# Moving the rotary tables, the decays' sums and two gate columns in a hybrid decoder layer

## The chip, the cores and the metric

The kernel runs on one core of a Trainium2 chip. The metric is device time in microseconds (us) of one execution; lower is better. A core has five engines that work in parallel, each through a queue of its own in order: TensorE (PE: matmuls, with weight loads PEld), VectorE (DVE), ScalarE (ACT), GpSimd (POOL) and SyncE (SP), which here issues the DMA transfers. They wait for each other by semaphores. SBUF is the memory on the chip, PSUM the small memory into which TensorE writes, DRAM the large one outside.

## The reference

One layer on 1024 tokens of width 1024, in float32:

```
h = rms_norm(x, norm_w)
a_q, a_k, a_v, a_gate, b_q, b_k, b_v, b_gate, b_low, m_a, m_b = split(h @ w_in)
o_a = sliding_window_attention(rope(a_q), rope(a_k), a_v, sinks) * silu(a_gate)
y_a = o_a @ w_a_proj
log_a = log_sigmoid(b_low @ b_gate_up + b_gate_bias) / 16
o_b = gated_linear_attention(b_q, b_k, b_v, log_a)    # chunks of 64
y_b = (rms_norm(o_b, b_out_norm_w) * silu(b_gate)) @ w_b_proj
merged = sigmoid(m_a) * y_a + sigmoid(m_b) * y_b
out = rms_norm(x + merged @ w_out, final_norm_w)
```

In linear attention the queries are multiplied by exp of the running sum of log_a in a chunk, and the keys by exp of minus that sum.

## The kernel before

**Matmuls.** Every float32 operand is split into a high part (`fp32r`, a cast on ACT, L117) and a low part (a subtraction, L118, mostly on POOL), and a product is three matmuls per block of 128: high x high, high x low, low x high (`half_product`, L129). A *column* below is 128 columns of a weight. One column over all 1024 tokens is done either directly (`m_tiles`, L332: two halves of 512 tokens, 8 blocks, 3 matmuls: 48 matmuls of 128x512), or two columns together as a *pair* (`pair`, L598, and `seven_products`, L455), after Strassen and Winograd: seven products of 12 matmuls, 84, in place of 96. A pair adds and subtracts blocks of the raw weights on DVE first (the pre-adds, L467 to L470), then casts (ACT) and subtracts (POOL) each combination, while products 1, 2 and 6 use raw blocks. Products go to six PSUM banks `sj`; DVE and ACT add them up (c, u: L489, L506, L515, L531), and `emit` finishes a block. For the right-hand side, the pair needs four sums of blocks of the tokens' matrix, T1 to T4, split by `t_split` (L287).

**The order of the program.** A scheduler moves instructions within limits by its own model of time; `tc.issue_after(x)` forbids issuing before x, and `tc.high_priority` puts work ahead. By stages:

1. Token tiles (L210): norm, transposes, splits; beside them the first columns 0 to 2 of the merge gate A (`O_MA`). `rstd_of` (L144) makes 1/sqrt(ss/n + eps) with two POOL instructions: a scaling, and a power of -0.5.
2. T splits, the low-rank product `low` (L355), and column 3 of merge gate A directly (`m_tiles([3])`, L377).
3. Pairs (L640 to L653). First four of merge gate B (`O_MB`), each with the decay gates of a head (`log_gate`, L576: log-sigmoid on ACT, a scan on DVE, L590), whose running sums go to DRAM, `sp_cum` (L595). Behind the second pair's gates the rotary tables are traced (`rotary_tables`, L383): some 40 steps of 128x256 on DVE, two sines on ACT, twelve stores to `sp_rope`. Then the pairs of q and k of linear attention (each with a load of the sums, an exp on ACT, L630, into one of four buffers `gt`, and a multiplication on POOL, L631), of the gate and of the values.
4. Attention. Its outputs go to DRAM, `sp_oa`.
5. Linear attention by steps (`gla_step`, L881, one head and 128 tokens each): `gla(0)` for two heads, then `gla(2)`. Beside them stand *fillers*, independent matmuls for a waiting TensorE: columns 4 to 7 of merge gate A, of which two run at attention's end and two in `gla(0)`. The list `pace` ties each group of three filler matmuls to a step. In the same stretch attention's outputs are read back (`oraw`) and split.
6. Both projections. That of linear attention is four turns k of seven products; `merge` (L1084) makes the merged blocks c11 to c22 at their end, and these are split (`split_block`, L976) as right-hand sides `mt` of the last product, the first being mt[0] = c21.
7. The output projection, residual, and last norm (`finish`, L1107).

Of the kernel before, what the change touches and what calls it, by code (L numbers as in the profile page):

```python
# [69 lines left out]
def layer_kernel(ctx: ExitStack, tc: tile.TileContext, consts, x, positions, norm_w, w_in, a_sinks,  # L70
# [30 lines left out]
    sp_cum = spill.tile([BH * BK, T], F32, name="sp_cum")  # L101
# [42 lines left out]
    def rstd_of(pool, ss, n, width):  # L144
        r = pool.tile([P, width], F32, name="rstd")
        nc.gpsimd.tensor_scalar(r, ss, 1.0 / n, EPS, ALU.mult, ALU.add)  # L146
        nc.gpsimd.tensor_tensor(r, r, mhalf[:, :width], ALU.pow)
        return r
# [21 lines left out]
    mhalf = const.tile([P, 8], F32, name="mhalf")  # L170
# [115 lines left out]

    def t_split(i, tag):  # L287

        m = [tph.tile([P, 4, 512], F32R, name=f"t{i}h"), slot(tpl if tag else tph, tag or "tl")]
        r = tr[i - 1]  # L290
        for k in range(4):
            nc.scalar.copy(m[0][:, k, :], r[:, k, :])
            nc.vector.tensor_sub(m[1][:, k, :], r[:, k, :], f(m, 0, k))
        return m
# [46 lines left out]
    fillers = list(range(4, 8))  # L341
# [25 lines left out]
    caus = const.tile([P, P], I32, name="caus")  # L367
    nc.vector.tensor_copy(caus, le)
# [206 lines left out]
    decays = [mwork, sctx.enter_context(pool_of(name="ex", bufs=2))]  # L575
    def log_gate(hd, th):  # L576
# [5 lines left out]
        gx = up_.tile([P, 512], F32, name="u3")  # L582
# [12 lines left out]
        nc.sync.dma_start(sp_cum[hd * BK : hd * BK + BK, sl], gx)  # L595
        return scan.ins
# [19 lines left out]
    def keep(sp, row, mode=None):  # L616
        def emit(c, a, th, b):
# [7 lines left out]
            elif mode in ("up", "down"):  # L625
                decays.reverse()
                t = decays[0].tile([P, 512], F32, name="gt")
                r = row + a * P
                nc.sync.dma_start(t, sp_cum[r : r + P, th * 512 : th * 512 + 512])
                nc.scalar.activation(t, t, AF.Exp, scale=1.0 / 16.0 if mode == "up" else -1.0 / 16.0)  # L630
# [305 lines left out]
    pace += [steps[min(15, 2 + i // 2)] for i in range(16 * len(fillers))]  # L936
# [39 lines left out]
    def split_block(m, k, r):  # L976
        nc.scalar.copy(m[0][:, k, :], r)
        nc.vector.tensor_sub(m[1][:, k, :], r, f(m, 0, k))  # L978
# [72 lines left out]
    def sums(i):  # L1051
# [11 lines left out]
        if i == 6:  # L1063
            split_block(mt[0], 3, c21[3])
            sum_row(3)
            split_block(mt[5], 3, t1s[3])
        if i == 7:
# [110 lines left out]
```

## Time and profile before

| | us |
|---|---|
| runs of the kernel | 1079.79, 1079.21, 1076.34; median 1079.21 |
| profiled execution | 1076.43 |
| its span in the trace | 1074.6 |
| TensorE busy | 1027.0 (96%) |
| VectorE busy | 756.3 (70%) |
| ScalarE busy | 540.8 (50%) |
| GpSimd busy | 507.3 (47%) |

The time of an execution is the span of the trace and a little around it. Busy time counts an engine's instructions; a TensorE that is busy need not be at its peak, since its clock can be granted at half rate, which the rows by stretch show as "PEclk" (1.00 is full). In a row of waits, "A <- B" means that A's engine was idle before A until B was done.

### The profile page before, as it was taken

The numbers are of one execution on the slowest core, as the hardware profiler recorded it, in microseconds if no ns is written. First come the engines' busy times: TensorE is split into PE (matmuls) and PEld (weight loads), VectorE is DVE, ScalarE is ACT, GpSimd is POOL, SyncE is SP. The second block draws the span as 40 slices with busy tenths as digits, with TensorE's granted clock in tenths as the row PEclk, the third lists the DMA queues.
The fourth block names the chain that finished last, engine by engine and source line by source line (L and its number), as shares of the span: only waits on it lengthen the run. The fifth ranks groups of instructions, "written<-read, shape, count | busy, mean of one in ns | idle before, by whom it ended". The sixth has DMA issues, their size and how long they took to land.

```text
span 1074.6 us, 16232 instructions
## 1 busy us (share of the span) xinstructions
PE 1027.0 (96%) x5572; PEld 872.0 (81%) x5572; DVE 756.3 (70%) x1315; ACT 540.8 (50%) x1321; POOL 507.3 (47%) x438
## 2 busy tenths in 40 slices
PE   7999998989999999999999999989989999997996
PEld 5788866867889998888888888878778887786996
DVE  6984797444665332379988787878856388899786
ACT  6535576333343223466766667647655244244445
POOL 3034444778897444766678676747843100000002
PEclk9999999989999999999999999999999999999999
DMA  8413343444333317222222222429764388442415
GB/s 275 113 59 108 128 137 123 153 141 136 101 109 108 118 40 216 59 59 59 71 59 59 78 71 76 140 84 303 244 222 158 115 268 256 136 140 97 167 52 194
DMA packets 126260, 140.54 MB, mean 131 GB/s; under 512 B 10337, under 2 KB 87009, under 8 KB 126178
## 3 DMA queue, kind: packets, MB, share of 16 engines
q1 hardware_dynamic: 126178, 139.51, 41.1%
q8 instruction: 44, 0.72, 0.3%
q14 instruction: 38, 0.31, 0.1%
HBM read 94.52 MB, written 40.24 MB: 125 GB/s over the span
## 4 chain that ended last, share of the span: by engine, by line
PE 61%; DVE 9%; POOL 2%; ACT 2%; issue 2%; DMA 2%; SPq 0%; POOLq 0%; DVEq 0%; ACTq 0%
PE pj L134 25%; PE sj L134 13%; PE sj L452 13%; PE sc L765 2%; PE av L805 2%; PE av L849 2%; PE pt L789 1%; DVE b L978 1%; PE sc L849 1%; PE av L889 1%; DMA oraw<-sp_oa 1%; PE av L890 1%; PE pt L922 1%; DVE wl L118 1%; DVE sm L788 1%
## 5 line engine op out<-in xcount | busy, mean ns | idle before, releaser
L134 PE MATMUL pj<-o,wh 128*128 128x512 f32 x1072 | 348.2, 399 | 2.2 <-DVE o L228 1.6
L134 PEld LDWEIGHTS pj<-o,wh 128*128 128x128 f32 x1072 | 198.7, 190 | 42.9 <-DVE o L228 2.0
L134 PE MATMUL pj<-o,wl 128*128 128x512 f32 x536 | 213.2, 398 | 0.0
L118 POOL TENSOR_TENSOR wl<-sraw,wh 128x512 fp32r<-128x512 f32 (+1 forms) x98 | 155.5, 1604 | 111.8 <-ACT wh L117 105.1
L134 PEld LDWEIGHTS pj<-o,wl 128*128 128x128 f32 x536 | 101.1, 189 | 21.0
L134 PE MATMUL sj<-o,wh 128*128 128x512 f32 x352 | 111.2, 395 | 1.6 <-DVE o L489 0.8
L117 ACT CAST wh<-wr 128x1024 fp32r<-128x1024 f32 (+1 forms) x76 | 66.4, 890 | 78.4 <-PE sj L452 22.4
L117 ACT CAST wh<-sraw 128x512 fp32r<-128x512 f32 (+1 forms) x98 | 63.4, 678 | 83.7 <-PE sj L134 22.4
L146 POOL TENSOR_SCALAR rstd<-zs 128x1 f32<-128x1 f32 x8 | 2.7, 334 | 210.1 <-DVE zs L1110 209.7
L118 POOL TENSOR_TENSOR wl<-wr,wh 128x1024 fp32r<-128x1024 f32 x26 | 64.1, 2467 | 66.4 <-ACT wh L117 66.4
L506 DVE TENSOR_TENSOR u<-u,sj 128x512 f32<-128x512 f32 x48 | 32.9, 685 | 68.8 <-PE sj L134 35.6
L134 PEld LDWEIGHTS sj<-o,wh 128*128 128x128 f32 x352 | 65.7, 187 | 18.2 <-ACT u L515 1.3
L134 PE MATMUL sj<-o,wl 128*128 128x512 f32 x176 | 69.4, 394 | 0.0
L452 PE MATMUL sj<-wh,b 128*128 128x256 f32 x320 | 60.8, 291 | 6.0 <-DVE b L978 4.2
L134 PE MATMUL sj<-t,wh 128*128 128x512 f32 x144 | 57.6, 400 | 0.0
L489 DVE TENSOR_TENSOR c<-u,sj 128x512 f32<-128x512 f32 x48 | 32.7, 682 | 34.9 <-PE sj L134 10.5
L452 PEld LDWEIGHTS sj<-wh,b 128*128 128x128 f32 x320 | 51.8, 199 | 6.7 <-DVE b L978 4.4
L452 PE MATMUL sj<-wh,o 128*128 128x256 f32 x320 | 55.9, 278 | 1.3 <-DVE o L569 1.3
L780 ACT ACTIVATE sm<-sc,nm 128x129 f32<-128x129 f32 x128 | 45.8, 369 | 22.5 <-DVE nm L776 22.1
L797 POOL TENSOR_TENSOR ch<-ph,cst 128x512 fp32r<-128x512 f32 x32 | 37.1, 1158 | 40.4 <-ACT ph L796 32.9
L118 DVE TENSOR_TENSOR wl<-wr,wh 128x512 fp32r<-128x512 f32 (+1 forms) x50 | 45.4, 924 | 14.3 <-ACT wh L117 14.2
L452 PEld LDWEIGHTS sj<-wh,o 128*128 128x128 f32 x320 | 48.8, 188 | 1.6 <-DVE o L569 1.5
(316 smaller groups left out, 2707.0 us busy)
## 6 DMA issues: line engine op xcount, KB each, us to landing
sraw<-in_w_in_dram SPq DMA_DIRECT2D x32, 512.0 KB, 3.9
wr<-in_w_in_dram SPq DMA_DIRECT2D x26, 512.0 KB, 3.9
r<-sp_ob SPq DMA_DIRECT2D x28, 256.0 KB, 4.3
qs<-q SPq DMA_DIRECT2D x72, 64.0 KB, 2.0
xt<-in_x_dram SPq DMA_DIRECT2D x8, 512.0 KB, 8.1
sp_ma<-gt SPq DMA_DIRECT2D x16, 256.0 KB, 2.4
sp_mb<-c SPq DMA_DIRECT2D x16, 256.0 KB, 2.0
gt<-sp_cum SPq DMA_DIRECT2D x16, 256.0 KB, 3.4
```

Of the source, the lines that this page charges most:

```text
L117: nc.scalar.copy(h, raw)
L118: rest[0].tensor_sub(l, raw, h.bitcast(F32))
L134: nc.tensor.matmul(p, a[:, k, :], b[:, k, :], start=start and k == 0 and y == 0, skip_group_check=True, stop=stop and k == 3 and y == 2)
L452: nc.tensor.matmul(p, m[i][:, k, t * P : t * P + P], w[j][:, k, :], start=start and k == 0 and y == 0, skip_group_check=True, stop=stop an ...
L489: nc.vector.tensor_add(o, like(u[i][b], o), like(x[j][b], o))
L506: nc.vector.tensor_add(o[b], u[i][b], x[j][b])
L765: nc.tensor.matmul(s[:, h * 256 : h * 256 + 256], lq, kk[kv][x][:, k0 : k0 + 2, :].rearrange("p n t -> p (n t)"), start=x == 0, stop=x == 1)
L780: nc.scalar.activation(sm[:, j, :], sel[j // 2][:, j % 2, :], AF.Exp, bias=nm[:, j : j + 1], accum_out=den[:, j : j + 1])
L788: nc.vector.tensor_scalar_mul(sm[:, j, :P], sm[:, j, :P], den[:, j : j + 1])
L797: nc.gpsimd.tensor_mul(ch, ph.bitcast(F32), leb)
L805: nc.tensor.matmul(av[:, b * 256 : b * 256 + 256], val[:, blk, kv, :], part[:, 2 * b : 2 * b + 2, :], start=y == 0, stop=y == len(terms) - 1)
L849: nc.tensor.matmul(p, a[i], b[j], start=start and y == 0, stop=stop and y == 2)
```

## The change

- **Rotary tables.** They are issued after the last of the T splits, so in DVE's queue they stand at the first pair; their pool is freed there.
- **Decays' sums.** They stay in SBUF (`cum0` to `cum3`). Eight stores and sixteen loads go, and so does the second pool of `gt` buffers: two are left of four.
- **Merge gate A.** `m_tiles([3])` goes; the fillers are columns 3, 4 and 5 (two at attention's end, one in `gla(0)`), and columns 6 and 7 are a pair between the pairs of merge gate B and those of q and k. Direct matmuls ahead of attention: 48 fewer; a pair's: 84 more; fillers: 192 to 144. `low` is traced ahead of three half columns. `pace` advances by 3/4 of a step for each filler group rather than 1/2.
- **rstd.** The scaling is folded into the square's scale and an extra column that holds eps, for the token tiles and for the last norm; linear attention keeps it.
- **The mask.** `caus` is the bits of `le` in place of a cast.
- **End of the b projection (k = 3).** The merge of c21 and the split of mt[0] get high priority; the merge of c22 and the splits of mt[6] are issued after that split.

```
@@
-    def rstd_of(pool, ss, n, width):
-        r = pool.tile([P, width], F32, name="rstd")
-        nc.gpsimd.tensor_scalar(r, ss, 1.0 / n, EPS, ALU.mult, ALU.add)
-        nc.gpsimd.tensor_tensor(r, r, mhalf[:, :width], ALU.pow)
+    def power(pool, ss):
+        r = pool.tile([P, 1], F32, name="rstd")
+        nc.gpsimd.tensor_tensor(r, ss, mhalf, ALU.pow)
         return r
@@
+        for xt in xts:
+            nc.gpsimd.memset(xt[:, D:], (EPS * D) ** 0.5)
@@
-            nc.scalar.activation(junk, xt, AF.Square, accum_out=ss)
-            r = rstd_of(xp, ss, D, 1)
+            nc.scalar.activation(junk, xt, AF.Square, scale=D**-0.5, accum_out=ss)
+            r = power(xp, ss)
@@
-            nc.vector.tensor_sub(m[1][:, k, :], r[:, k, :], f(m, 0, k))
+            last_split.append(nc.vector.tensor_sub(m[1][:, k, :], r[:, k, :], f(m, 0, k)).ins)
@@
-    fillers = list(range(4, 8))
+    fillers = [3, 4, 5]
@@
-    caus = const.tile([P, P], I32, name="caus")
-    nc.vector.tensor_copy(caus, le)
+    caus = le.bitcast(I32)
@@
-    m_tiles([3])
@@
+    with tc.issue_after(last_split[-1]):
+        rotary_tables()
@@
-    decays = [mwork, sctx.enter_context(pool_of(name="ex", bufs=2))]
+    cums = gctx.enter_context(pool_of(name="cum", bufs=1, side="right"))
+    cum = [cums.tile([P, T], F32, name=f"cum{i}") for i in range(BH)]
@@
-        gx = up_.tile([P, 512], F32, name="u3")
+        gx = cum[hd][:, sl]
@@
-        nc.sync.dma_start(sp_cum[hd * BK : hd * BK + BK, sl], gx)
@@
-                decays.reverse()
-                t = decays[0].tile([P, 512], F32, name="gt")
-                r = row + a * P
-                nc.sync.dma_start(t, sp_cum[r : r + P, th * 512 : th * 512 + 512])
-                nc.scalar.activation(t, t, AF.Exp, scale=1.0 / 16.0 if mode == "up" else -1.0 / 16.0)
+                t = mwork.tile([P, 512], F32, name="gt")
+                nc.scalar.activation(t, cum[row // P + a][:, th * 512 : th * 512 + 512], AF.Exp, scale=1.0 / 16.0 if mode == "up" else -1.0 / 16.0)
                 nc.gpsimd.tensor_mul(c, c, t)
@@
-        if c == 2:
-            with tc.issue_after(scan):
-                rotary_tables()
+    pair(O_MA + 6 * P, P, keep(sp_ma, 6 * P, "tanh"))
@@
-    pace += [steps[min(15, 2 + i // 2)] for i in range(16 * len(fillers))]
+    pace += [steps[min(15, 2 + i * 3 // 4)] for i in range(16 * len(fillers))]
@@
-            split_block(mt[0], 3, c21[3])
+            with tc.high_priority(offset=400):
+                first.append(split_block(mt[0], 3, c21[3]))
+            with tc.issue_after(first[0]):
+                late.pop()()
@@
-            for k in range(4):
-                split_block(mt[6], k, c12[k])
+            with tc.issue_after(first[0]):
+                for k in range(4):
+                    split_block(mt[6], k, c12[k])
@@
         def merge(o, a, th, b):
+            if (k, a, th) == (3, 1, 1):
+                late.append(lambda: merge_block(o, a, th))
+                return
+            with tc.high_priority(offset=400) if (k, a, th) == (3, 1, 0) else nullcontext():
+                merge_block(o, a, th)
+
+        def merge_block(o, a, th):
@@
-    ssq = zw.tile([P, NT, 4], F32, name="ssq", bufs=1)
+    ssq = zw.tile([P, NT, 5], F32, name="ssq", bufs=1)
+    nc.gpsimd.memset(ssq[:, :, 4], EPS)
```

How the queue of VectorE reads in the third pair before (pre-adds of the weights `sraw`, sums c and u of the pair, and steps of the tables between them):

```order
L467 TENSOR_TENSOR sraw<-sraw 128x4x128
L531 TENSOR_TENSOR c<-u_1248,u_1283 128x512
L398 TENSOR_SCALAR rnd<-turns 128x256
L468 TENSOR_TENSOR sraw<-sraw 128x4x128
L506 TENSOR_TENSOR u_1214<-u_1214,sj 128x512
L489 TENSOR_TENSOR c<-u_1283,sj 128x512
L399 TENSOR_SCALAR rnd<-rnd 128x256
L469 TENSOR_TENSOR sraw<-sraw 128x4x128
L400 TENSOR_TENSOR turns<-turns,rnd 128x256
```

In that place only pre-adds, sums and gates are left. VectorE's queue now, at the start of the first pair, right behind the splits (the last step of `low`, then the pair's pre-adds, and the tables' `ang`, `dig` and `turns`):

```order
L382 CAST ang<-pos 128x256
L365 TENSOR_TENSOR low<-av,low 32x512
L470 TENSOR_TENSOR sraw<-sraw 128x4x128
L383 TENSOR_SCALAR ang<-ang,cst 128x256
L471 TENSOR_TENSOR sraw<-sraw 128x4x128
L387 TENSOR_SCALAR dig_709<-ang 128x256
L472 TENSOR_TENSOR sraw<-sraw 128x4x128
L388 TENSOR_SCALAR dig_709<-dig_709 128x256
L473 TENSOR_TENSOR sraw<-sraw 128x4x128
L389 SCALAR_TENSOR_TENSOR ang<-dig_709,ang 128x256
```

The tables' first steps moved between the first pair's pre-adds, and most of the others stand ahead of the pair's first c.

VectorE's queue before at the end of the b projection, where the last blocks are merged (`o_9490` is c12, `o_9492` c22, `o_9491` c21, `o_9489` c11) and split:

```order
L1091 TENSOR_TENSOR o_9492<-o_9492,yt 128x512
L978 TENSOR_TENSOR b_10153<-o_9492,b_10152 128x512
L1091 TENSOR_TENSOR o_9491<-o_9491,yt 128x512
L489 TENSOR_TENSOR o_9490<-u_10091,sj 128x512
L118 TENSOR_TENSOR wl<-wr,wh 128x1024
L978 TENSOR_TENSOR o_10216<-o_9490,o_10215 128x512 x3
L978 TENSOR_TENSOR b_10181<-o_9489,b_10180 128x512
L1090 SCALAR_TENSOR_TENSOR o_9490<-ym,o_9490 128x512
L978 TENSOR_TENSOR b_10038<-o_9491,b_10037 128x512
```

The last of these rows is the split of mt[0]. The same place now, with other numbers of the tiles (`o_9480` is c12, `o_9482` c22, `o_9481` c21, `o_9479` c11; the split of mt[0] is `b_10028`):

```order
L1103 TENSOR_TENSOR o_9481<-o_9481,yt 128x512
L977 TENSOR_TENSOR b_10137<-o_9482,b_10136 128x512
L492 TENSOR_TENSOR o_9480<-u_10081,sj 128x512
L117 TENSOR_TENSOR wl<-wr,wh 128x1024
L977 TENSOR_TENSOR b_10165<-o_9479,b_10164 128x512
L1102 SCALAR_TENSOR_TENSOR o_9480<-ym,o_9480 128x512
L977 TENSOR_TENSOR b_10028<-o_9481,b_10027 128x512
L1102 SCALAR_TENSOR_TENSOR o_9482<-ym,o_9482 128x512
L977 TENSOR_TENSOR o_10206<-o_9480,o_10205 128x512 x3
L470 TENSOR_TENSOR wr<-wr 128x1024
```

The three splits of `o_10206` (mt[6]) and the two merge steps of `o_9482` moved from ahead of mt[0]'s split to behind it.

More of the change, by code (lines that the diff above doesn't have):

```diff
@@ L98, in layer_kernel @@
     psum["pj"] = pj
-    sp_cum = spill.tile([BH * BK, T], F32, name="sp_cum")
     sp_oa = spill.tile([D, T], F32, name="sp_oa")
@@ L169, in layer_kernel @@
     le = cst[:, C_LE : C_LE + P]
-    mhalf = const.tile([P, 8], F32, name="mhalf")
+    mhalf = const.tile([P, 1], F32, name="mhalf")
     nc.gpsimd.memset(mhalf, -0.5)
@@ L191, in layer_kernel @@
         nc.vector.memset(ones[:, :1], 1.0)
-        xts = [xp1.tile([P, D], F32, name=f"xt{t}") for t in range(NT)]
+        xts = [xp1.tile([P, D + 1], F32, name=f"xt{t}") for t in range(NT)]
+        for xt in xts:
+            nc.gpsimd.memset(xt[:, D:], (EPS * D) ** 0.5)
         def load(t):
-            nc.sync.dma_start(xts[t], x[t * P : (t + 1) * P, :])
+            nc.sync.dma_start(xts[t][:, :D], x[t * P : (t + 1) * P, :])
         load(0)
@@ L211, in token_tile @@
             xt = xts[t]
-            junk = xp.tile([P, D], F32, name="junk", bufs=1)
+            junk = xp.tile([P, D + 1], F32, name="junk", bufs=1)
             ss = xp.tile([P, 1], F32, name="ss")
-            nc.scalar.activation(junk, xt, AF.Square, accum_out=ss)
-            r = rstd_of(xp, ss, D, 1)
+            nc.scalar.activation(junk, xt, AF.Square, scale=D**-0.5, accum_out=ss)
+            r = power(xp, ss)
             ps = []
@@ L285, in f @@
         return m[y][:, k, :].bitcast(F32)
+    last_split = []
     def t_split(i, tag):
@@ L365, in layer_kernel @@
             nc.vector.tensor_sub(low[o + 32 : o + 64, sl], p[0:32, :], low[0:32, sl].bitcast(F32))
-    caus = const.tile([P, P], I32, name="caus")
-    nc.vector.tensor_copy(caus, le)
+    for c in range(3):
+        m_half(c, w_first[c], 1)
+    t4, t2, t3, t1 = (t_split(*y) for y in ((4, None), (2, "t4"), (3, "t2"), (1, "t3")))
+    caus = le.bitcast(I32)
     up = const.tile([P, 2, P], I32, name="up")
@@ L424, in rotary_tables @@
                 nc.sync.dma_start(sp_rope[i, :, g * 256 : g * 256 + 256], trig[i][g * 32 : g * 32 + 32, :])
+    with tc.issue_after(last_split[-1]):
+        rotary_tables()
+    rctx.close()
+    tctx.close()
+    c1.close()
     slots = []
@@ L1038, in layer_kernel @@
     t1s, t2s = [], []
+    first, late = [], []
     def sum_row(k):
@@ L1142, in norm @@
                 junk = zw.tile([P, 256], F32, name="zj", bufs=1)
-                nc.scalar.activation(junk, o[:, t, :], AF.Square, accum_out=ssq[:, tok, 2 * h + a : 2 * h + a + 1])
+                nc.scalar.activation(junk, o[:, t, :], AF.Square, scale=D**-0.5, accum_out=ssq[:, tok, 2 * h + a : 2 * h + a + 1])
                 if h == 1 and a == 1 - th:
```

20 lines of the change are left out of this document (7 added, 13 removed).

## The prediction

> **What bounds the kernel now.** I read the totals first, then the chain, then busy time by stretches, and last the waits and the timeline inside the stretches that stood out. The page's totals (busy time, share of the span, instructions) and two pieces of the chain of work that ended last (start, length, what):
>
> ```profile
> span 1074.6 us, 16232 instructions
> PE 1027.0 (96%) x5572; PEld 872.0 (81%) x5572; DVE 756.3 (70%) x1315; ACT 540.8 (50%) x1321; POOL 507.3 (47%) x438
> ...
> 243.38 88.00 PE sj L134 x382
> 410.52 22.39 PE pj L134 x96
> ```
>
> TensorE is busy for 96% of the span, and the chain is mostly runs of 128x512 matmuls that issue every 88.00/382 = 0.230 to 22.39/96 = 0.233 us. So there are two ways to gain: fewer matmuls where TensorE is full, or fewer stalls where it isn't. The stretches tell the two apart. Columns: stretch, its length, then busy time (instructions) of PE, PEld, DVE, ACT, POOL, then the granted clock, the DMA share, GB/s.
>
> ```profile
> 60.00:80.00 20.00, 20.00 (x88) 16.13 (x87) 15.65 (x18) 4.49 (x8) 5.14 (x4) 1.00 0.16 52
> 80.00:100.00 20.00, 20.00 (x89) 16.33 (x88) 6.78 (x11) 8.25 (x15) 10.17 (x8) 1.00 0.30 93
> 100.00:120.00 20.00, 20.00 (x89) 16.32 (x88) 13.52 (x17) 11.89 (x19) 7.79 (x6) 1.00 0.46 145
> ...
> 140.00:160.00 20.00, 17.59 (x73) 13.15 (x72) 19.97 (x32) 14.57 (x22) 8.14 (x6) 1.00 0.35 114
> 160.00:180.00 20.00, 15.45 (x58) 11.50 (x57) 14.52 (x27) 15.44 (x24) 8.08 (x8) 0.92 0.40 131
> ...
> 200.00:220.00 20.00, 19.24 (x83) 15.05 (x81) 10.09 (x12) 6.79 (x12) 14.18 (x11) 1.00 0.53 167
> 220.00:243.00 23.00, 20.76 (x77) 16.38 (x77) 9.69 (x11) 8.35 (x15) 15.51 (x12) 0.85 0.43 138
> ...
> 700.00:720.00 20.00, 17.67 (x102) 14.66 (x101) 14.08 (x38) 8.94 (x28) 8.28 (x7) 1.00 0.29 93
> ```
>
> TensorE is full in the first three, loses time from 140 to 180 and from 200 to 243 (the later pairs of the merge gate B and the first pairs of q and k), and loses a little in linear attention (from 700). The change touches these places, and the merge of the b projection near 985 us.
>
> **The change part by part.** The sum is made on the profiled execution, which took 1076.43 us (span 1074.6 and 1.8 around it), 2.8 below the median of the three runs, 1079.21.
>
> *Matmuls moved.* Column 3 of the merge gate A, 48 matmuls, leaves the full stretch between the splits and the first pair; columns 6 and 7 arrive there as a pair of 84 (seven products of 12). That is 36 more at 0.233 us: **+8.4 us**. It is certain as far as TensorE is full there, which the pairs from 80 to 120 us are.
>
> *Rotary tables.* From 140 to 160 us DVE is busy 19.97 of 20 us, while gates, pre-adds and tables share it. Who waited, from 140 to 180 us (total, times, longest), and TensorE's timeline (start, length, idle before it):
>
> ```profile
> POOL wl L118 <- ACT wh L117: 21.7, 7, 5.2
> PE sj L134 <- POOL wl L118: 3.1, 4, 2.0
> ...
> 174.15 0.50 PE L134 MATMUL sj<-t2h,wh 128*128 128x512 f32 x1 [2.32 <-ACT wh L117]
> ...
> 176.93 0.79 PE L134 MATMUL sj<-t2h,wl 128*128 128x512 f32 x1 [2.04 <-POOL wl L118]
> ```
>
> DVE's late pre-adds make ACT's cast late, then POOL's subtraction, then TensorE. Idle TensorE in the two stretches is 2.41 + 4.55 = 7.0 us. Behind the two gaps the clock falls:
>
> ```profile
> 176.80:180.20 3.40, 3.27 (x8) 2.60 (x9) 1.40 (x3) 3.37 (x6) 0.40 (x2) 0.51 0.56 159
> 221.20:228.00 6.80, 5.87 (x14) 4.63 (x15) 0.69 (x1) 2.14 (x5) 4.58 (x4) 0.50 0.88 280
> ```
>
> 3.4 us at half clock is 1.7 us lost: 8.7 in all. By the count of matmuls, 131 where full stretches have 89 each, it is 47 x 20/89 = 10.6. I take **-9.5**. The pair from 100 to 120 us, which has decay gates and no tables, shows what is left without them: nothing. The Trainium skill (TensorE: Matmul & The Clock Gate, "HAM oscillation — how this bites in real kernels") warns only of idle gaps above about 3.4 us; the gaps here were 2.32 and 2.04 us and the clock still fell, so the trace decides. By the page the term would be 1.7 smaller.
>
> The tables now go into DVE's queue among the pre-adds of the first pair, which starts about 11 us earlier since column 3 no longer stands ahead. Their price is seen in DVE's groups from 130 to 170 us (busy, mean ns); the dearest group, a middle one and the cheapest are:
>
> ```profile
> L392 DVE SCALAR_TENSOR_TENSOR ang<-dig,ang 128x256 f32<-128x256 f32 x3 | 2.3, 754 | 0.1
> ...
> L400 DVE TENSOR_TENSOR turns<-turns,rnd 128x256 f32<-128x256 f32 x3 | 1.2, 408 | 0.0
> ...
> L385 DVE CAST ang<-pos 128x256 f32<-128x256 int32 x1 | 0.3, 261 | 0.0
> ```
>
> The 33 steps there sum to 15.7 us; two sines and a table load on ACT go with them. What room there is in the first pair, from the timelines (TensorE's first matmul of the pair, then DVE), with the page's group of ACT's casts and one of POOL's subtractions from the chain:
>
> ```profile
> 80.15 0.63 PE L134 MATMUL sj<-o,wh 128*128 128x512 f32 x2
> ...
> 67.40 2.40 DVE L293 TENSOR_TENSOR t<-t,t1h 128x512 fp32r<-128x512 f32 x2
> ...
> 86.02 0.69 DVE L489 TENSOR_TENSOR c<-u,sj 128x512 f32<-128x512 f32 x1 [10.05 <-PE sj L134]
> 91.41 0.69 DVE L506 TENSOR_TENSOR u<-u,sj 128x512 f32<-128x512 f32 x1 [4.70 <-PE sj L134]
> ...
> L117 ACT CAST wh<-sraw 128x512 fp32r<-128x512 f32 (+1 forms) x98 | 63.4, 678 | 83.7 <-PE sj L134 22.4
> ...
> 242.04 1.30 POOL wl L118
> ```
>
> 10.05 + 4.70 us of waiting for TensorE nearly hold them. The first product made of pre-adds is the fourth, 36 x 0.233 = 8.4 us into a pair that starts at 69: at 77.4. It needs three of the four, and in the order a table step stands ahead of each, so the third ends at about 69.8 (the splits' end) + 3 x (0.69 + 0.33) = 72.9; a step of the low part (0.7) makes it 73.6, and cast and subtraction 75.6: 1.8 us to spare. (0.33 lies between the steps' 0.261 and 0.408.) The step c (L489), which came 5.9 us after the pair's start at 80.15, gets 19 table steps and those pre-adds ahead of it, 6.3 + 2.8 + 0.7 us behind the splits: 79.6, where its data are there at about 74.9. It comes some 5 us late; TensorE has six sj banks and misses c's at the eighth product, 19.6 us in; but the copy, the table of sines and the casts behind it on ACT can be late by that. I take 1.5 us of stall (0 to 15.7, all the tables in the open): **+1.5**. SyncE's twelve stores of the tables stand behind two loads of weights and ahead of the next; they wait for the sines, so the third pair's weights issue later; the stretch at 80 to 100 has DMA at 0.30, so I cost that at nothing, and if the cover fails it is inside the 15.7.
>
> *Decays' sums in SBUF.* The waits from 200 to 245 us and ACT's timeline:
>
> ```profile
> ACT gt L630 <- DMA gt<-sp_cum: 17.0, 7, 4.7
> ACT wh L117 <- DVE sraw L468: 9.8, 2, 5.8
> ...
> 208.71 0.63 ACT L630 ACTIVATE gt<-gt 128x512 f32<-128x512 f32 x1 [2.25 <-DMA gt<-sp_cum]
> ```
>
> ACT works in order, so an exp that waits for a load from DRAM holds up the casts behind it, then POOL, then TensorE. TensorE idles 0.76 + 2.24 = 3.0 us there and runs 6.8 us at half clock (3.4 lost): 6.4. The loads go; but exp now has two buffers, not four, and its third instance waits for POOL's multiplication of the first. POOL is busy 14.18 of 20 us, so it is near its limit, and what is queued behind a waiting exp is again the casts. I leave 1.4 of stall: **-5.0** (0 to -6.4).
>
> *Linear attention.* It had two columns beside its first half, now one: 48 matmuls fewer, at most 11.2 us. For the stretch of twelve steps, the stretch row, TensorE's two groups of fillers, and one wait:
>
> ```profile
> 722.90:770.30 47.40, 45.63 (x281) 38.67 (x280) 36.88 (x97) 34.98 (x107) 35.55 (x48) 1.00 0.86 283
> ...
> L134 PE MATMUL pj<-o,wh 128*128 128x512 f32 x56 | 18.9, 412 | 0.0
> ...
> L134 PE MATMUL pj<-o,wl 128*128 128x512 f32 x28 | 11.1, 395 | 0.0
> ...
> ACT o L953 <- DMA oraw<-sp_oa: 9.5, 6, 2.6
> ```
>
> 84 fillers at 0.233 are 19.6 of the 47.4 us, and TensorE is the fullest engine, with DVE 36.88 behind it. Were TensorE the only bound, all 11.2 would come back; were the chain of one step, DVE or the loads (DMA share 0.86) the bound, nothing would. With DVE 10.5 us below the stretch, and each step a chain across four engines, I take about half: **-6.0** (0 to -11.2). Three of the oraw loads are now issued earlier, during attention, where they stand in SyncE's queue behind attention's stores; the row from 700 shows DMA at 0.29, so I cost that at nothing.
>
> *End of the b projection.* DVE and TensorE on the timeline:
>
> ```profile
> 986.08 1.90 DVE L978 TENSOR_TENSOR o<-o,o 128x512 fp32r<-128x512 f32 x3
> ...
> 989.09 0.70 DVE L978 TENSOR_TENSOR b<-o,b 128x512 fp32r<-128x512 f32 x1
> 993.16 1.24 DVE L118 TENSOR_TENSOR wl<-wr,wh 128x1024 fp32r<-128x1024 f32 x1
> ...
> 989.84 0.58 PE L452 MATMUL sj<-wh,b 128*128 128x256 f32 x1 [4.19 <-DVE b L978]
> ```
>
> In the order now, that split (the last of mt[0]) has five steps fewer ahead of it: three splits of mt[6] (1.9 us) and two steps of the merge of c22 (1.2). So TensorE resumes 3.0 us earlier. But the same steps then stand ahead of the next weight's low part, which came at 994.4 (the order still puts the same work ahead of it) and which TensorE needs 34 matmuls later, about 4 us at full clock (256 columns, so half of 0.233 each); TensorE may wait a second time there and lose its clock again. I take **-1.0** (-4.5 if the second wait stays away, +2 if it costs the clock once more).
>
> *The rstd step.* POOL's scaling goes at the eight token tiles and the eight finishes; it is kept in linear attention.
>
> ```profile
> L146 POOL TENSOR_SCALAR rstd<-zs 128x1 f32<-128x1 f32 x8 | 2.7, 334 | 210.1 <-DVE zs L1110 209.7
> ...
> DVE xt L220 <- POOL rstd L147: 6.9, 2, 4.1
> ```
>
> Only the first and the last tile are in the open, 0.3 us each: **-0.5** (0 to -1). The mask's cast is hidden: nothing.
>
> Sum: 8.4 - 9.5 + 1.5 - 5.0 - 6.0 - 1.0 - 0.5 = -12.1, so 1064.3 on the profiled execution's scale and 1067.1 on the median's. I forecast **1065.5 us**.
>
> **The rivals.** (a) *Everything comes back*: linear attention gives 11.2, no stall is left in the first pair or at the exps: 1065.5 - 5.2 - 1.5 - 1.4 = 1057.4. For it: TensorE is full from 100 to 120 us. Against: the waits of linear attention are many and small. (b) *Linear attention gives nothing*, because its steps, not TensorE, set the pace: 1065.5 + 6.0 = 1071.5. For it: from 700 to 720, with 17.67 of 20 us busy, TensorE already waits. (c) *The exps' wait moves to POOL*: with two buffers the casts are as late as before: 1065.5 + 5.0 = 1070.5. For it: POOL's 14.18 and 15.51 us. (d) *It doesn't do what it says*: gates and pre-adds alone fill DVE in the third pair, and the stalls of 140 to 180 stay: 1065.5 + 9.5 = 1075.0; b or c with it is no change. Against: 100 to 120 us. (e) *Slower*: the tables stand in the open in the first pair. They are 15.7 us of DVE in a place where TensorE has just lost its 11 us of cover (column 3), and the clock falls behind the stall. It decides from the point where the pre-adds are more than 1.8 us later than I reckon, so that the fourth product waits, and all the steps queued behind them on DVE with it. Price 15.7 - 1.5 plus 3.4 for two stretches at half clock: 1065.5 + 17.6 = 1083.1. Against: only four table steps stand among the pre-adds, and DVE idles 14.75 us there.
>
> **How the numbers follow.** Forecast 0.52, a 0.12, b 0.12, c 0.08, d 0.07, e 0.09. The range 1056 to 1076 holds all but e, part of d and the tail of a. About 0.3%, 3.2 us, is what a measurement of this kernel tells from no change. Faster by more: the forecast, a, b, c and a little of d, taken down slightly for unknown costs, 0.83. Within it: most of d, 0.08. Slower: e, 0.09.
>
> **What would show it.** Right: TensorE 20 of 20 us in the stretches of the third and fourth pair, clock 1.00 there; no half-clock stretch at the first q and k pairs; DVE idle under 5 us in the first pair; the steps of linear attention about 0.5 us closer; TensorE's resumption at mt[0]'s split 3 us sooner, and a wait for a low part 34 matmuls on. Wrong: gaps of TensorE over 2 us before the second pair; exps of ACT waiting for POOL with casts behind them and TensorE idle; linear attention of the same length with TensorE less busy.

## The result and the profile after

| | before | after |
|---|---|---|
| median of the runs, us | 1077.78 (4 runs, 1074.71 to 1079.79) | 1068.01 (4 runs, 1067.16 to 1069.02) |
| span of the profiled execution, us | 1074.6 | 1066.2 |

The ratio is 0.9912, 95% interval 0.9884 to 0.9941: the change makes the kernel 0.9% faster, 2.5 us short of the forecast of 1065.5. To see where the 8.4 us of span come from, the program is cut at four of TensorE's instructions: the first product of the first pair (`sj`), the first product behind the pairs (`pj`), the first step of linear attention, and the first product of its projection. From TensorE's timelines (start, length), first before and then after; the first of before is in the prediction (80.15), whose 410.52 is where a piece of the chain starts, 0.16 us behind the first product:

```profile
410.36 0.62 PE L134 MATMUL pj<-o,wh 128*128 128x512 f32 x2
...
711.65 0.33 PE L888 MATMUL av<-bq,bk 128*128 128x64 f32 x2
...
878.55 0.62 PE L134 MATMUL sj<-b,wh 128*128 128x512 f32 x2
```

```profile
67.51 0.63 PE L133 MATMUL sj<-o,wh 128*128 128x512 f32 x2
...
406.50 0.62 PE L133 MATMUL pj<-o,wh 128*128 128x512 f32 x2
...
710.48 0.53 PE L886 MATMUL av<-bq,bk 128*128 128x64 f32 x2
...
871.46 0.86 PE L133 MATMUL sj<-b,wh 128*128 128x512 f32 x3
```

| stage | before | after | difference | forecast |
|---|---|---|---|---|
| to the first pair | 80.15 | 67.51 | -12.64 | -11.2 (column 3) and half of -0.5 |
| pairs | 330.21 | 338.99 | +8.78 | +19.6 (84 matmuls) -9.5 +1.5 -5.0 = +6.6 |
| attention | 301.29 | 303.98 | +2.69 | 0 |
| linear attention, beginning of the projections | 166.90 | 160.98 | -5.92 | -6.0 |
| the rest | 196.05 | 194.74 | -1.31 | -1.0 and half of -0.5 |

With 84 matmuls at the forecast's 0.233 us, 10.8 us of stalls went from the pairs, where 13.0 were forecast. In the first stage, about 1.7 of the 12.64 us are a stretch at half clock that before has (0.91 granted from 40 to 60 us) and after has not (1.00). What is left in the pairs shows in the busy time by stretch of the kernel after (PE, PEld, DVE, ACT, POOL, granted clock, DMA share, GB/s):

```profile
60.00:80.00 20.00, 19.52 (x85) 15.57 (x84) 19.67 (x29) 11.41 (x19) 12.74 (x8) 1.00 0.20 66
80.00:100.00 20.00, 20.00 (x89) 16.34 (x88) 19.45 (x36) 11.70 (x18) 6.50 (x5) 1.00 0.42 126
100.00:120.00 20.00, 18.93 (x83) 15.13 (x82) 14.36 (x21) 14.88 (x25) 10.17 (x9) 1.00 0.32 106
120.00:140.00 20.00, 19.02 (x83) 15.24 (x82) 14.44 (x19) 10.74 (x18) 8.83 (x6) 1.00 0.24 74
140.00:160.00 20.00, 18.21 (x78) 14.20 (x77) 15.86 (x21) 11.99 (x21) 10.55 (x8) 1.00 0.28 99
160.00:180.00 20.00, 17.97 (x77) 14.40 (x78) 14.18 (x19) 10.77 (x17) 8.80 (x7) 1.00 0.29 93
180.00:200.00 20.00, 20.00 (x89) 16.32 (x88) 10.91 (x14) 8.42 (x16) 15.40 (x12) 1.00 0.37 118
200.00:220.00 20.00, 20.00 (x89) 16.33 (x88) 9.76 (x11) 8.50 (x15) 18.06 (x14) 1.00 0.39 122
```

VectorE is full from 60 to 100 us, as the tables there made likely, and TensorE loses nothing by it in the first pair. From 180 us on TensorE is full, where it lost 6.4 us before. But from 100 to 180 us it is idle for 1.07 + 0.98 + 1.79 + 2.03 = 5.9 us, in pairs that have gates and no tables. The waits from 100 to 180 us, and below them one of the whole kernel:

```profile
POOL wl L117 <- ACT wh L116: 41.6, 12, 6.0
ACT u L518 <- DVE cum L598: 13.8, 3, 5.0
...
PE sj L133 <- ACT u L518: 3.4, 3, 1.4
...
PE sj L133 <- POOL wl L117: 2.5, 2, 1.4
```

```profile
ACT gt L630 <- POOL c L631: 34.0, 13, 4.5
```

The last row is the rival with two exp buffers: exp does wait for GpSimd, 34.0 us in 13 waits, and TensorE is full all the same. The other rows name two chains, and ScalarE's timeline in the second pair shows both (start, length; `u<-pj` and `u<-u` are the gates, `wh` the casts of weights):

```profile
113.89 0.68 ACT L590 ACTIVATE u<-pj,gbias 128x512 f32<-128x512 f32 x1
...
115.56 1.14 ACT L592 ACTIVATE u<-u 128x512 f32<-128x512 f32 x2
116.72 1.28 ACT L593 ACT_TABLE_LOAD   x1
...
119.08 1.12 ACT L116 CAST wh<-sraw 128x512 fp32r<-128x512 f32 x2
125.20 1.07 ACT L518 COPY u<-sj 128x512 f32<-128x512 f32 x2 [5.00 <-DVE cum L598]
```

The gates' work with a table load of 1.28 us stands between casts; then the copy of the next pair's first product waits 5.00 us until VectorE has finished the gates, because `log_gate` takes its scratch from the same two `u1` buffers. TensorE's side of the two: at 116.86 us it had waited 1.06 us for GpSimd's `wl`, and at 125.84 us 0.98 us for ScalarE's `u`.

### The profile page after: what moved, and what is told of

It is laid out like the page before. It is cut to its first block, busy times and chain, and to the rows that moved or that the text cites. A ratio compares the mean times of both kernels' runs of the same rounds, so it can differ in the third digit from the quotient of the medians.

```text
span 1066.2 us, 16206 instructions
## 1 busy us (share of the span) xinstructions
PE 1020.7 (96%) x5560; PEld 867.8 (81%) x5560; DVE 759.5 (71%) x1325; ACT 542.6 (51%) x1328; POOL 509.3 (48%) x436
## 4 chain that ended last, share of the span: by engine, by line
PE 72%; DVE 11%; ACT 5%; DMA 4%; issue 3%; POOL 3%; SPq 1%; POOLq 0%; DVEq 0%; ACTq 0%
PE pj L133 25%; PE sj L133 24%; PE sj L455 13%; PE sc L763 2%; PE av L803 2%; PE av L847 2%; POOL wl L117 1%; DMA xt<-in_x_dram 1%; DVE b L977 1%; DVE u L595 1%; PE pt L787 1%; ACT wh L116 1%; PE av L887 1%; DVE wl L117 1%; DVE sm L786 1%
## 5 line engine op out<-in xcount | busy, mean ns | idle before, releaser
L133 PE MATMUL pj<-o,wh 128*128 128x512 f32 x1008 | 327.7, 399 | 2.9 <-DVE o L229 2.1
L117 POOL TENSOR_TENSOR wl<-sraw,wh 128x512 fp32r<-128x512 f32 (+1 forms) x105 | 163.7, 1576 | 141.1 <-ACT wh L116 131.7
L133 PEld LDWEIGHTS pj<-o,wh 128*128 128x128 f32 x1008 | 186.7, 190 | 41.2 <-DVE o L229 2.5
L133 PE MATMUL pj<-o,wl 128*128 128x512 f32 x504 | 200.3, 398 | 0.0
L133 PE MATMUL sj<-o,wh 128*128 128x512 f32 x376 | 120.1, 399 | 3.4 <-ACT u L518 3.4
L133 PEld LDWEIGHTS pj<-o,wl 128*128 128x128 f32 x504 | 95.4, 189 | 19.5
L116 ACT CAST wh<-sraw 128x512 fp32r<-128x512 f32 (+1 forms) x105 | 67.5, 673 | 69.8 <-PE sj L133 21.4
L133 PEld LDWEIGHTS sj<-o,wh 128*128 128x128 f32 x376 | 71.0, 190 | 21.7 <-ACT u L518 4.6
L117 POOL TENSOR_TENSOR wl<-wr,wh 128x1024 fp32r<-128x1024 f32 x24 | 58.7, 2444 | 35.5 <-ACT wh L116 35.5
L133 PE MATMUL sj<-o,wl 128*128 128x512 f32 x188 | 74.9, 398 | 0.0
```

The source lines that it names most:

```text
L116: nc.scalar.copy(h, raw)
L117: rest[0].tensor_sub(l, raw, h.bitcast(F32))
L133: nc.tensor.matmul(p, a[:, k, :], b[:, k, :], start=start and k == 0 and y == 0, skip_group_check=True, stop=stop and k == 3 and y == 2)
```

## The experiments

Times are medians with their runs' range; each ratio is against the kernel before, run beside it. The intervals hold the spread of before as well, so close kernels are told apart better by the ranges. "After" is 1068.0 (1067.2 to 1069.0; 0.9912). It was not run again beside the experiments, which ran in three groups (t1, c1, s1, g1; g2, e1, e2, l1; g3, s2, b1, b2); before's medians there were 1078.0, 1078.2 and 1079.1. One run of g2 took 2557.16 us, for no reason that is known; it is left out of its median, range and ratio (the 1063.7 of the expectations is the median with it), and b1, which contains g2, has no such run.

| run | what | us | ratio, 95% interval |
|---|---|---|---|
| t1 | before, with the tables moved alone | 1075.1 (1070.7 to 1078.3) | 0.9965, 0.9947 to 0.9984 |
| c1 | after, gate columns as before | 1066.5 (1063.6 to 1069.8) | 0.9898, 0.9872 to 0.9925 |
| s1 | after, sums through DRAM | 1078.8 (1077.1 to 1082.3) | 1.0017, 1.0003 to 1.0030 |
| g1 | after, gates' own scratch | 1069.9 (1069.0 to 1071.4) | 0.9933, 0.9916 to 0.9951 |
| g2 | after, gates one pair later, own scratch | 1063.2 (1063.0 to 1064.3) | 0.9880, 0.9843 to 0.9918 |
| g3 | after, gates one pair later | 1068.9 (1068.0 to 1069.8) | 0.9904, 0.9868 to 0.9939 |
| s2 | s1 with the gates one pair later | 1081.2 (1079.2 to 1083.7) | 1.0019, 0.9998 to 1.0039 |
| e1 | after, end of the b projection as before | 1068.4 (1067.4 to 1068.9) | 0.9923, 0.9899 to 0.9948 |
| e2 | after, last low parts on GpSimd | 1076.8 (1074.1 to 1079.7) | 0.9991, 0.9973 to 1.0008 |
| l1 | after, attention's outputs loaded later | 1066.9 (1064.8 to 1069.1) | 0.9911, 0.9883 to 0.9939 |
| b1 | g2 and l1 | 1064.0 (1063.2 to 1065.1) | 0.9859, 0.9823 to 0.9895 |
| b2 | b1, gate columns as before | 1068.8 (1066.6 to 1069.5) | 0.9899, 0.9862 to 0.9936 |

The theory at first: the tables kept VectorE full, and without them the pairs with gates alone have no stall. Its rival: the gates hold up ScalarE whether tables stand there or not.

**t1: the tables moved alone.**

```
-        if c == 2:
-            with tc.issue_after(scan):
-                rotary_tables()
+    with tc.issue_after(last_split[-1]):      # behind m_tiles([3])
+        rotary_tables()
```

> The kernel before with one part of the change: the rotary tables issued behind the last T split; column 3 still stands there as cover. Theory: the tables alone fill DVE in the second and third pair, so TensorE's lost time from 140 to 180 us (9.5 us with the half clock) falls to about 3, and the first pair shows no stall: 1078 - 6.5 = 1071, with 1069 to 1073 in keeping. Rival: the decay gates hold up the casts there through the two u1 buffers that they share with the pair's copies, tables or none: gain under 3, 1075 to 1078.

Measured: 1075.1, -0.35% or 3.8 us by the ratio, 2.9 by the medians. That is in the rival's range, at its edge. The stretches of t1, whose profile is of the slowest of its ten executions (1078.3):

```profile
140.00:160.00 20.00, 18.37 (x78) 14.00 (x76) 11.48 (x15) 11.36 (x20) 8.54 (x6) 1.00 0.38 119
160.00:180.00 20.00, 17.64 (x75) 14.11 (x76) 15.00 (x21) 13.54 (x22) 10.47 (x8) 1.00 0.39 132
...
180.00:260.00 80.00, 73.74 (x309) 58.37 (x309) 41.29 (x51) 28.60 (x51) 56.43 (x42) 0.98 0.45 142
```

The last stretch before:

```profile
180.00:260.00 80.00, 76.62 (x318) 61.26 (x317) 43.51 (x51) 27.94 (x50) 57.52 (x42) 0.96 0.45 142
```

From 140 to 160 us VectorE fell from 19.97 to 11.48 us, and TensorE is still idle 1.6 us there and 2.4 in the next stretch. That VectorE was full was true, and it was not the whole reason for TensorE's waits. The half clock of 176.8 to 180.2 us is gone (1.00 in both). And part of what the move gained was lost further on: at the first pairs of q and k, from 180 to 260 us, TensorE is idle 6.3 us in t1 and 3.4 before, and gets only 1.7 us of it back by the clock (0.98 granted against 0.96). The whole range of t1 is wide, so the 0.35% is worth no more than its interval.

**g1, g2, g3: the gates.** g1 changes one name, g3 moves the calls, g2 does both.

```
-        ge = up_.tile([P, 512], F32, name="u1")
+        ge = up_.tile([P, 512], F32, name="u3")          # g1, g2
@@
-        for th in range(TH):
-            log_gate(c // 2, th)
+        for th in range(TH if c else 0):                  # g2, g3
+            log_gate(c // 2 - 1, th)
     pair(O_MA + 6 * P, P, keep(sp_ma, 6 * P, "tanh"))
+    for th in range(TH):
+        log_gate(3, th)
```

> The changed kernel with the decay gates' scratch taken from the u3 buffers, which the gates no longer use, in place of the u1 buffers that the pair's first copy needs. Theory: TensorE's stalls of 1.1 to 1.6 us at the pairs' ends from 100 to 180 us (6.6 in all) come from ACT's copy of u1 waiting until the gates release the buffer; three or more of the five go: 1068 - 4 to 1068 - 6.6, 1061.4 to 1064. Rival: ACT is late because of the gates' own work and its table loads, whatever the buffer: 1068 within 1.5.

g1 measured 1069.9: no gain, so the buffer alone isn't it. The stalls at the pairs' ends did go, and others came in the second pair and once at 163.83 us, each place with 3.4 us at half clock behind it. ScalarE's timeline of g1 in the second pair, and TensorE's rows:

```profile
90.82 1.28 ACT L592 ACT_TABLE_LOAD   x1
...
92.76 1.28 ACT L593 ACT_TABLE_LOAD   x1
...
94.71 1.28 ACT L622 ACT_TABLE_LOAD   x1
...
96.54 1.12 ACT L116 CAST wh<-sraw 128x512 fp32r<-128x512 f32 x2
```

```profile
97.71 0.50 PE L133 MATMUL sj<-t2h,wh 128*128 128x512 f32 x1 [1.71 <-ACT wh L116]
...
163.83 0.50 PE L133 MATMUL sj<-t2h,wl 128*128 128x512 f32 x1 [2.05 <-POOL wl L117]
```

With its buffer free earlier, the first gate's work is ordered right behind the last rotary sine, with three table loads in a row, and the casts come behind all of it, at 96.54 us, where after has them at 91.87. The prediction's slower rival looked for such a stall in the first pair and on VectorE's queue; here it is in the second, and on ScalarE's.

> The changed kernel with each head's decay gates behind the pair after (the first pair has none, the gate columns 6 and 7 have the last head's), and with the gates' scratch in the u3 buffers. Theory: the stalls left in the pairs come from ACT, where the gates' work with its table loads stands ahead of the casts of the next weights, worst where the rotary sines come on top; apart from each other both fit in: of 6.6 us of stalls from 100 to 180 us 4 or more go, 1068 - 4 to 1068 - 6.6, 1061.4 to 1064. Rival: the gates only carry their stalls with them into the later pairs: 1068 within 1.5.

> As g2 (each head's gates one pair later), but the gates' scratch stays in the u1 buffers. Theory: the place of the gates' work in ScalarE's queue is what counts, so this is g2 within 1.5: 1062.2 to 1065.2. Rival: the shared buffers hold up the pairs' first copies: two or three stalls of 1.2 to 1.5 us are back, 1066 to 1068.

g2 measured 1063.2, 4.9 us below after; g3 1068.9. Stretches of g2, then of g3:

```profile
100.00:120.00 20.00, 20.00 (x88) 16.33 (x88) 17.23 (x21) 17.05 (x25) 10.64 (x8) 1.00 0.39 122
...
180.00:200.00 20.00, 17.82 (x78) 14.17 (x77) 13.92 (x14) 7.27 (x13) 17.00 (x12) 1.00 0.23 82
200.00:220.00 20.00, 20.00 (x89) 16.33 (x88) 10.73 (x12) 8.46 (x15) 16.82 (x13) 1.00 0.50 154
```

```profile
180.00:200.00 20.00, 17.06 (x71) 12.55 (x69) 15.57 (x19) 8.04 (x13) 14.12 (x10) 1.00 0.19 66
200.00:220.00 20.00, 18.08 (x68) 14.48 (x68) 8.73 (x11) 8.49 (x15) 17.51 (x14) 0.83 0.40 121
```

With both edits TensorE is full from 60 to 180 us and loses 2.2 us once. With the place alone the stalls move to 180 to 220 us, and the clock falls as well. So it takes both, and my guess for g3 (the place is what counts) fell: the shared buffers count as much. From 60 to 220 us ScalarE's copy waits for the gates in g3 again (12.6 us in 3 waits), in g2 not once. Run beside g3, b1 (g2's edits and a later load) is 4.9 us below it, and the ranges are apart. VectorE is at 17.23 us and ScalarE at 17.05 in g2's stretch from 100 us, and TensorE is full.

**s1, s2: the sums.**

```
-        gx = cum[hd][:, sl]
+        gx = up_.tile([P, 512], F32, name="u3")          # stored to sp_cum at the end
@@
-                t = mwork.tile([P, 512], F32, name="gt")
-                nc.scalar.activation(t, cum[...], AF.Exp, ...)
+                decays.reverse()                           # 2 + 2 buffers
+                t = decays[0].tile([P, 512], F32, name="gt")
+                nc.sync.dma_start(t, sp_cum[...])
+                nc.scalar.activation(t, t, AF.Exp, ...)
```

> The changed kernel with the decays' sums stored to DRAM and loaded again, and four exp buffers, as before. Theory: the waits of exp on loads return at the first q and k pairs with the half clock: 5 to 6.4 us, 1073 to 1074.4. Rival: exp waits for POOL now (34.0 us of waits in the profile after) as long as it waited for loads, and TensorE is full for another reason: 1068 within 1.5.

Measured: 1078.8, 10.8 us above after and no better than before. The waits of s1 from 195 to 265 us, and its stretches:

```profile
ACT gt L634 <- DMA gt<-sp_cum: 24.2, 7, 4.7
```

```profile
200.00:220.00 20.00, 19.00 (x84) 15.18 (x83) 6.07 (x7) 6.05 (x11) 13.90 (x11) 1.00 0.43 132
220.00:240.00 20.00, 16.60 (x71) 12.97 (x70) 8.61 (x12) 7.20 (x13) 13.92 (x12) 1.00 0.50 158
240.00:260.00 20.00, 18.57 (x81) 14.81 (x80) 10.57 (x12) 6.67 (x12) 16.04 (x12) 1.00 0.46 145
```

TensorE is idle 1.00 + 3.40 + 1.43 = 5.8 us at the first pairs of q and k, where after has none: the theory's 5 to 6.4. The rest I put down to a late cast in the second pair, as in g1, and s2 was to take that away with the gates' place. The cast is late in s1 too, but for another reason: the gates' scan stands ahead of a pre-add in VectorE's queue, and the cast waits for that pre-add. TensorE waits 1.96 and 1.02 us there, with 3.4 us at half clock behind:

```profile
94.38 2.08 DVE L595 TENSOR_TENSOR_SCAN u<-run,u 128x512 f32<-128x512 f32 x1
...
97.08 0.62 ACT L117 CAST wh<-sraw 128x512 fp32r<-128x512 f32 x1 [1.89 <-DVE sraw L473]
```

> The changed kernel with the sums through DRAM and four exp buffers, as in s1, and with each head's gates one pair later, as in g2 (scratch in u1). Theory: s1's loss of 10.8 us is two things, the exps' waits for loads (5 to 6.4) and a late cast in the second pair, where the gates' work on ScalarE came between the rotary sines and the casts (3.3 us of stalls at 95 to 100 us and 1.7 at half clock); with the gates later only the first is left: g3 + 5 to g3 + 6.5. Rival: the sums' stores and loads cost all of it, whatever the gates' place: g3 + 9 to g3 + 11.

Measured: 1081.2 against g3's 1068.9, 12.2 us: the rival. The second pair is full in s2, and more is lost further on: from 180 to 260 us TensorE is busy 69.87 of 80 us at a granted clock of 0.94 (75.14 and 0.96 in g3), and exps wait for loads there 26.5 us in 8 waits. The sums' way through DRAM costs 11 to 12 us in the changed kernel, whichever way the gates stand. That is the price of the whole edit: stores, loads, buffers and the sums' scratch in `u3` were not tried apart.

**c1, b2: the gate columns.**

```
-    fillers = [3, 4, 5]
+    fillers = list(range(4, 8))
+    m_tiles([3])                                          # ahead of the tables
-    pair(O_MA + 6 * P, P, keep(sp_ma, 6 * P, "tanh"))
-    pace += [steps[min(15, 2 + i * 3 // 4)] ...]
+    pace += [steps[min(15, 2 + i // 2)] ...]
```

> The changed kernel with the gate columns as before: column 3 direct behind the splits, 4 to 7 as fillers, no pair, pace as before. Theory: 36 matmuls go from the full stretch (-8.4) and the 5.9 us that linear attention gave come back: 1068 - 8.4 + 5.9 = 1065.5, so this part of the change is a loss by itself. Rival: linear attention loses the full price of 48 matmuls, 11.2: 1068 - 8.4 + 11.2 = 1070.8.

Measured: 1066.5, the theory's number within 1 us. The ranges of c1 and after overlap, so it is not shown that the pair is a loss by itself, only that it gains nothing. In the profiles c1 is 10.3 us shorter than after up to the end of the pairs, and 5.0 longer in linear attention and 4.0 behind it, with a wait of 4.12 us for a cast at the end of the b projection that after doesn't have.

> b1 with the gate columns as before the change (column 3 direct, 4 to 7 as fillers, no pair; the last head's gates in the first pair of q). Theory: the pair costs 8.4 us where TensorE is full and gives back 5 to 6 in linear attention, so without it 1.6 (c1) to 3 less: b1 - 1.6 to b1 - 3. Rival: the pair's stretch is where the last gates fit in; without it their work meets the exps of the first q and k pairs: b1 or above.

Measured: 1068.8, 4.8 above b1: the rival. Without the pair the last gates run beside the exps of the first q and k pairs, and the stretch from 180 us shows TensorE as in g3:

```profile
180.00:200.00 20.00, 16.63 (x65) 12.97 (x64) 14.02 (x20) 9.08 (x16) 13.85 (x11) 0.91 0.29 92
```

By the stages of the profiles, b2 is still 4.2 us shorter than b1 up to the end of the pairs, where 36 matmuls fewer are worth 8.4, and it is 6.4 longer in linear attention and 3.9 behind it. So the stalls in the pairs explain about 4 us of the difference, and the rest lies in the later stages. What the pair is worth depends on what is put beside it: nothing that can be told in after, some 5 us with the gates one pair later.

**e1, e2: the end of the b projection.** e1 undoes the order (no priority, no `late`, splits of mt[6] where they were). e2:

```
+    rest[0] = nc.gpsimd
     for h in range(2):
         w = {}
```

> The changed kernel with the end of the b projection as before: no priority for the last split of mt[0], merge of c22 and splits of mt[6] where they were. Theory: what the first wait lost was given back at the next weights' casts, so little comes back: 1068 + 1.25, 1067.5 to 1070. Rival: the saved wait was worth its 3 to 4 us and the clock stretch behind it, and the later waits have other causes: 1071 to 1073.

Measured: 1068.4, so the edit is worth nothing that can be told. TensorE's timeline of after shows idle times of 0.44, 1.62 and 1.65 us where before had 4.19. In e1 they are 3.00, 0.55 and 1.40, which is 1.2 us more, but no half clock follows, where after has it from 986.8 to 990.2 us and loses 1.7. So in these two profiles the clock took what the first wait gave back:

```profile
979.73 0.38 PE L455 MATMUL sj<-wh,b 128*128 128x256 f32 x1 [0.44 <-DVE b L977]
...
984.96 0.73 PE L455 MATMUL sj<-wh,o 128*128 128x256 f32 x4 [1.62 <-ACT wh L116]
...
987.35 0.58 PE L455 MATMUL sj<-wl,o 128*128 128x256 f32 x1 [1.65 <-DVE wl L117]
```

> The changed kernel with the low parts of the output projection's weights subtracted on GpSimd, which idles there, in place of VectorE. Theory: VectorE is full from 960 to 996 us and sets TensorE's waits there (6.8 us and about 3 us more at half clock); without some five low parts of 1.2 us on it half of that goes: 1062.5 to 1065. Rival: GpSimd takes 2.45 us for a low part and slows VectorE beside it, so the next weights come no sooner: 1068 to 1071.

Measured: 1076.8, 8.8 us slower: the rival, and dearer than it said. TensorE in e2:

```profile
994.76 0.58 PE L455 MATMUL sj<-wl,o 128*128 128x256 f32 x1 [8.01 <-POOL wl L117]
```

The low part that it waited for took GpSimd from 986.05 to about 994.7 us, while VectorE was busy all the time; of the five moved, the shortest took 2.82 us and the longest 8.96. VectorE takes 1.22 us for one in after. The expectation had reckoned with 2.45.

**l1, b1: attention's outputs loaded later.**

```
+                with tc.issue_after(steps[4 + th * 6]):
                     nc.sync.dma_start(raw, sp_oa[...])
```

> The changed kernel with the loads of attention's outputs held back, the first half behind the fifth step of linear attention, the second behind the eleventh. Theory: with fewer fillers the loads crowd into a shorter stretch (DMA share 1.02 from 760 to 768 us, where TensorE waits 3.0 us for a step's values); spread out, that wait and the half clock behind it go: 1068 - 3 to 1068 - 5. Rival: the loads are the longest chain in that stretch, and to hold them back makes the splits late for the next columns: 1068 to 1072.

> g2 with the loads of attention's outputs held back as in l1. Both gains lie in different stages and add: 1063.7 - 1 to 1063.7 - 3.7 (the stage of linear attention was 3.7 us shorter in l1's profile), 1060 to 1062.7. Rival: l1's difference was noise: 1063.7 within 1.

Measured: 1066.9 and 1064.0, no difference from after and from g2 that can be told. The test did not do what it was for. The 2.80 us wait of after is still there (2.81 in l1), DMA is as busy, and the wait is for VectorE's `ktl` (after's row); around its own, l1 has GpSimd busy 7.92 of 8.00 us and a DMA share of 1.03:

```profile
764.22 0.36 PE L847 MATMUL av<-vh,ath 128*128 128x256 f32 x1 [2.80 <-DVE ktl L842]
```

Whether GpSimd or the DMA makes VectorE late is left open.

## Why the prediction was right, and where its steps were off

The range and the sign held, and 1068.0 is 2.5 us above the forecast; between the profiled spans it is -8.4 where the sum said -12.1. Of its signs, the clock of 1.00 in the third and fourth pair, the full stretches at the first q and k pairs, VectorE's little idle time in the first pair and the second wait at the b projection came; a TensorE without idle time in the third and fourth pair did not. By its steps:

- **Matmuls moved, +8.4.** Right: c1 is 10.3 us shorter up to the end of the pairs, 2.0 of it in idle time, so 8.3 for the 36 matmuls. For this step and the next together, +2.4 was forecast and 1.6 measured in c1, with ranges that overlap.
- **Linear attention, -6.0.** The number was right, with 5.92 us less, and the ground for it was not. Half of the price was to stay because the chain of a step, VectorE or the loads would hold TensorE up. The stage before and after (PE, PEld, DVE, ACT, POOL, granted clock, DMA share, GB/s):

```profile
711.65:878.55 166.90, 159.79 (x904) 133.33 (x904) 111.34 (x276) 87.72 (x258) 74.31 (x109) 1.00 0.64 206
```

```profile
710.48:871.46 160.98, 153.50 (x857) 128.45 (x857) 108.31 (x276) 85.14 (x256) 73.05 (x108) 0.97 0.63 202
```

TensorE is idle 7.1 us before and 7.5 after, so the waits took nearly nothing. After runs some 10 us at half clock (from 710.3 to 717.2 and from 764.9 to 768.3 us, behind the waits of 1.86 and 2.80 us), and loses 5 us by it; before has none. Without that nearly the full 11.2 us would have come back. How much half clock falls here varies between profiles: 3.4 us are lost in t1, whose linear attention is that of before (169.8 us), and 1.7 in l1. So the agreement is luck in part.
- **Rotary tables, -9.5 + 1.5.** The first pair took them without a stall, as reckoned from VectorE's idle time: TensorE is busy 19.52 and 20.00 us (the missing 0.48 stands ahead of the pair), so the 1.5 wasn't needed and the slower rival didn't come. The -9.5 was wrong. The step that failed is "The pair from 100 to 120 us, which has decay gates and no tables, shows what is left without them: nothing." One pair without tables was taken for all. In t1, with the tables gone from there, 1.6 and 2.4 us of idle time are left in the two stretches, and the whole kernel gained 0.35%, some 3.8 us, part of the gain being lost again at the first pairs of q and k. What is left is ScalarE's: the gates' work and table loads ahead of casts, and the `u1` buffers. g2, which takes both away, finds 4.9 us.
- **Sums, -5.0 (0 to -6.4).** The direction and the place were right, the size was not: s1 and s2 put it at 11 to 12 us. The bound was read from the idle time and half clock at one place of before. In s1 the exps' place cost 5.8 us, as reckoned, and the second pair, where the queues had come into another order, 3.0 idle and 1.7 by the clock; in s2 some 7 us more than in g3 are lost from 180 to 260 us, idle time and clock together. A wait seen in one order is no bound for what it costs in another. Which part of the edit makes the difference is left open.
- **Exp waiting for GpSimd** came as named, 34.0 us, and cost nothing: TensorE is full from 180 us on.
- **End of the b projection, -1.0.** The mechanism was right, with the first wait down from 4.19 to 0.44 us and a second at the next weights of 1.62 and 1.65. The net, -1.3 in the profile with the last norm's part, is not to be told from nothing in e1.
- **Attention, 0.** It took 2.69 us more in the profile, part of it at its end (a wait of 1.86 us ahead of its last matmuls, where before has 1.12). Nothing there was changed but the loads that are issued early. The other profiles spread by as much: 302.5 us in t1, whose attention is that of before, and 302.1 to 305.8 with the change's. So a small loss is likely, and its cause is left open.

The two wrong sizes, of the tables and the sums, lean opposite ways: -8.0 forecast for the tables where alone they gave -3.8, -5.0 for the sums where they gave about -11. They don't add up to the whole, since t1 was measured in the kernel before and s1 in the kernel after: the stages share ScalarE's queue, and one part's gain depends on the others. That the total came near is partly luck.

## What to carry to other kernels

An engine that is full beside a stall is a suspect, not the cause: name what it makes late, and ask what else makes the same thing late. Here the cure was not fewer instructions but two edits that only help together (g2, 1063.2, ahead of both kernels): scratch that doesn't share its buffers with the chain, and a place in the in-order queue where nothing urgent stands behind. And when a step is moved, count its table loads on ScalarE: three of 1.28 us in a row made casts late that no dependence tied to them.

## What the runs showed of the hardware that was not expected

TensorE's clock fell behind short waits in some places and not in others, and the length of the wait doesn't tell which. A single gap of 2.18 us in g2 (195.71 to 197.89 us) left the clock at 1.00; a single gap of 2.05 us in g1 (161.78 to 163.83) was followed by 3.4 us at half clock. In each trace the moments at which the clock changes lie on one grid: they are multiples of 3.41 us apart (three half clocks of before begin at 176.9, 221.2 and 989.2 us, the later two 13 and 238 steps of 3.413 us behind the first). Cut along that grid, the stretches show what decides (busy TensorE first, granted clock third from the end; g2, then g3, then g1):

```profile
193.84:197.26 3.42, 1.87 (x9) 1.19 (x7) 0.69 (x1) 0.62 (x2) 3.42 (x4) 1.00 0.04 15
197.26:200.67 3.41, 2.78 (x12) 2.32 (x13) 0.17 (x1) 1.76 (x5) 3.39 (x4) 1.00 0.68 209
```

```profile
197.07:200.49 3.42, 1.58 (x6) 0.86 (x5) 1.25 (x2) 0.56 (x2) 3.42 (x3) 1.00 0.20 77
200.49:203.90 3.41, 1.98 (x5) 1.60 (x6) 0.00 (x0) 2.14 (x4) 3.39 (x4) 0.50 0.42 116
```

```profile
161.77:165.19 3.42, 1.37 (x7) 1.15 (x7) 1.25 (x2) 3.40 (x6) 2.01 (x2) 1.00 0.26 85
165.19:168.60 3.41, 3.41 (x10) 2.64 (x9) 2.44 (x3) 3.38 (x6) 1.37 (x2) 0.50 0.46 145
```

g2's gap falls across the edge of two steps and leaves both busy enough; g1's falls into one. In the pairs of all profiles here (60 to 330 us), the clock fell behind each of the ten full-clock steps with at most 1.58 us busy, and behind none with 1.60 or more. Where matmuls are smaller that bound doesn't hold: in linear attention the clock fell behind steps that were busier.

The Trainium skill (TensorE: Matmul & The Clock Gate, "What's actually happening") says that the clock is set by how busy TensorE was in a free-running window of about 3.4 us. The rows agree: what counts is the share of such a window, and not whether a gap is as long as the window.
